# Mixer output stage: stores moved from SyncE to ScalarE and one product later, weight loads one tile sooner, inputs loaded and split in pieces, R times q in place

## The chip, the cores and the metric

The kernel runs on one core of a Trainium2 chip. The metric is the device time in microseconds of one execution of the program on that core. The core has TensorE (PE, with its weight loads shown apart as PEld), VectorE (DVE), ScalarE (ACT), GpSimd (POOL) and SyncE (SP). Each engine works through its own instructions in the order in which the built program holds them. SP here only issues DMA transfers, in one queue that is served in order.

## The reference

One layer with 128 context tokens and 2048 latent tokens, 2176 tokens in all, of 1024 channels in float32:

```
h = rmsnorm(x, norm1) * (1 + scale1) + shift1
z = h @ w_in
sc_b, sc_c, sc_x, q, k, v, o, g = jnp.split(z, idx, axis=-1)
y_sc = sc_b * conv3(sc_c * sc_x)                     # 512 channels
h_m, C, n, m = mlstm_bidir(q, k, v, g, C0, n0, m0)   # 4 heads of 128, chunks of 128 tokens
h_m = rmsnorm(h_m) * mh_norm * jax.nn.sigmoid(o)
x = x + gate1 * (jnp.concatenate([y_sc, h_m], axis=-1) @ w_out)
h2 = rmsnorm(x, norm2) * (1 + scale2) + shift2
a, gg = jnp.split(conv3(h2 @ w_up), 2, axis=-1)
x = x + gate2 * ((jax.nn.silu(gg) * a) @ w_down)
y = rmsnorm(x, final_norm)
```

(The reshapes, the context and latent calls and the per-head details are left out.) The change lies in the third to seventh of these lines.

## The kernel before

**Tiles and products.** Channels lie on the 128 partitions, tokens along the free dimension. Tokens are cut into six blocks `BL` of 384 (the last of 256). A float32 product is made of three matmuls: weights and inputs are split into a high part (`wh`, `hH`) and a low part (`wl`, `hL`), and `gemm` adds wh·hH, wh·hL and wl·hH for eight tiles of 128 channels. One such product (24 matmuls, called a product below) makes 128 output channels for one block. `load_w` brings one weight tile of 128x1024 from HBM (tile `wst`, two buffers), ACT makes `wh` from it (L110) and POOL makes `wl`.

**The stages.** After the norm and the first projections come the gate phase, `Sums` (backward states), then `Mix`, the output projection, and the FFN, which is the larger half of the time. In `Mix` there are 34 units, one for each of 17 chunks and two pairs of heads, with these stages:

- `load`: k, v, q and the backward state sb, by DMA (L724, L729, L793).
- `rows`: one row of 1024 numbers from HBM spread over all partitions into tile R (L799; four buffers). Half of R (index 0) is made into the weight matrix W, the other half (index 1) holds factors for q.
- `pre`: POOL adds a mask to W (L805), ACT takes the exponential (L809, four pieces).
- `first`: PE makes the scores in tile S, DVE multiplies the factors with q into a tile qs (L819) and the scores into W (L820, written as R).
- `second`: o2 is loaded; PE makes y from qs and the state, and from W and v (L831 and L833). DVE brings the forward state sf on (L837), takes the denominators den (L841 to L843), and with ACT makes hv (L848, L849), its sum of squares (L851, into hss) and its norm (L855).
- `third`: PE transposes hv into tile st (L861), DVE multiplies it into o2, shown as o (L863).
- `last`: o2 is stored to HBM as rows 4 to 7 of yD (L868).

`weave` sets the order in code. One step handles a stage each of several units, and then takes one product from `fill`: the q and o heads, the short convolution (which stores rows 0 to 3 of yD), and then the output projection:

```
for k, stage in ((-1, "second"), (0, "first"), (-3, "third"), (-4, "last"), (1, "pre"), (1, "load"), (2, "rows")):
```

**The output projection** (`out_proj`) takes the blocks in groups (0,1), (2,3), (4,5), and in each group eight output tiles m. For each m and block: a product into `acc`, then DVE adds gate1 times acc to a row tile that was loaded with x (L459, six buffers `row`), SP stores the row to xD (L461), ACT squares it (L466) and DVE adds the square to a sum (L467), from which `stats` makes the norm. The rows of the next tile are asked for one tile ahead (L436); the weights are asked for two tiles ahead, in `load_w`, which issues the DMA and the split together. The inputs of the product, `early[b]`, come from `load_y`: two DMAs of four rows each (tile `xt`, two buffers) and eight splits each on ACT and DVE. It is called for blocks 0 and 1 by the short convolution (its argument `then`), for block 2 at m = 4, for block 4 at m = 7, and for blocks 3 and 5 after a product of m = 7.

**What sets the order.** The code is written in an order, but the framework fixes each engine's order at build time with a scheduler of its own that may move instructions past each other. All DMAs are issued by SP, so a store that waits for its data holds back the loads behind it. When the stages of Mix are at their end, the last 16 products of the projection run on beside the first column sums of the FFN (`sums`, tile F, L255).

## Time and profile before

| what | us |
|---|---|
| median of 3 runs | 2561.06 |
| the runs' range | 2560.59 to 2562.93 |
| the profiled execution | 2561.92 |
| its span (first to last instruction) | 2560.1 |

Busy time of the engines by stretch of the profiled execution, with the mean granted clock of PE (1.00 is full speed) and the share of time in which the DMA engines were busy:

| us of the span | what runs | PE | DVE | ACT | POOL | clock | DMA |
|---|---|---|---|---|---|---|---|
| 0 to 220 | modulation, first norm | 199.72 | 165.74 | 75.02 | 79.50 | 0.97 | 0.77 |
| 220 to 640 | projections, gate phase | 409.77 | 132.72 | 119.55 | 102.70 | 0.99 | 0.50 |
| 640 to 720 | up to the first Mix units | 80.00 | 28.84 | 24.89 | 19.73 | 1.00 | 0.57 |
| 720 to 830 | Mix beside short convolution | 109.19 | 66.51 | 58.55 | 42.50 | 1.00 | 0.73 |
| 830 to 1150 | Mix beside output projection, then the projection's end | 286.90 | 217.72 | 165.40 | 118.89 | 0.96 | 0.79 |
| 1150 to 2090 | FFN up, convolution | 926.77 | 697.03 | 483.94 | 185.64 | 0.99 | 0.32 |
| 2090 to 2560 | FFN down, final norm | 457.19 | 337.79 | 185.48 | 13.69 | 0.98 | 0.66 |

In rows of the trace, `PE y L833 <- DVE R L820: 14.7, 8, 5.0` says that PE's instruction of line 833, which writes y, waited for DVE's of line 820, which wrote R: 14.7 us in all, 8 times, 5.0 at most. `acc<-hH,wh` names the output tile and the inputs. In a row of the timeline the first two numbers are start and duration in us, x2 stands for two like instructions shown as one, and `[1.54 <-DVE R L820]` is the idle time of the engine ahead of it and who ended it. SPq is SP's queue.

### The profile page before, as it was taken

The page shows a single profiled execution, that of the slowest core. Times are in us where ns is not written, and L with a number is a line of the kernel's source. Part 1 is how long each engine was busy: PE and PEld are TensorE (multiplying, and loading weights), DVE is VectorE, ACT ScalarE, POOL GpSimd, SP SyncE. Part 2 cuts the span into 40 slices and gives each one's busy share as a digit, 9 for nine tenths or more (in the row PEclk, how much of TensorE's full clock was granted, in tenths as well). Part 3 has the DMA queues.
Part 4 walks back from the last instruction along what each step waited for, and adds up shares of the span by engine and source line. Part 5 has one row for each costly group of instructions (what it writes and reads, how often), then busy time and mean ns, then how long its engine had stood idle before and what let it go on. Part 6 is the DMA issues. An engine that isn't in the chain of part 4 may idle for free.

```text
span 2560.1 us, 42529 instructions
## 1 busy us (share of the span) xinstructions
PE 2469.5 (96%) x16127; PEld 2364.6 (92%) x16127; DVE 1646.4 (64%) x2741; ACT 1112.8 (43%) x2035; POOL 562.6 (22%) x470
## 2 busy tenths in 40 slices
PE   8997999999999889899999999899999999999998
PEld 7997999999999889899999999788888889999998
DVE  3995432322356666778678666877777786787586
ACT  3521133322245555455455444555555554444342
POOL 2442223211233443322122111211221200000000
PEclk9999999999999999999999999999999999999999
DMA  7778623356567787775225222422222286767674
GB/s 281 240 268 292 232 83 119 100 170 176 182 190 244 250 266 228 250 257 173 83 79 174 74 83 83 146 100 84 91 99 83 87 260 207 248 204 224 187 218 134
DMA packets 281423, 444.60 MB, mean 174 GB/s; under 512 B 23282, under 2 KB 206722, under 8 KB 279554
## 3 DMA queue, kind: packets, MB, share of 16 engines
q1 hardware_dynamic: 281218, 441.88, 53.0%
q8 instruction: 127, 2.08, 0.3%
q14 instruction: 78, 0.64, 0.1%
HBM read 335.31 MB, written 106.48 MB: 173 GB/s over the span
## 4 chain that ended last, share of the span: by engine, by line
PE 74%; DVE 9%; DMA 8%; issue 3%; POOL 2%; ACT 2%; SPq 1%; DVEq 0%; POOLq 0%; ACTq 0%
PE pa L1004 7%; PE pa L1006 6%; PE pa L1005 6%; PE d L1163 6%; PE d L1164 6%; PE d L1162 6%; PE acc L204 5%; PE acc L206 5%; PE acc L205 5%; PE pb L1004 3%; PE pb L1006 3%; PE pb L1005 3%; DVE y L528 3%; PE pc L1004 2%; PE pc L1005 2%
## 5 line engine op out<-in xcount | busy, mean ns | idle before, releaser
L204 PE MATMUL acc<-hH,wh 128*128 128x384 f32 (+1 forms) x1536 | 515.1, 335 | 23.1 <-DVE cr L391 12.0
L205 PE MATMUL acc<-hL,wh 128*128 128x384 f32 (+1 forms) x1536 | 507.1, 330 | 0.0
L206 PE MATMUL acc<-hH,wl 128*128 128x384 f32 (+1 forms) x1536 | 507.0, 330 | 0.0
L1162 PE MATMUL d<-bh,wh 128*128 128x272 f32 x1232 | 357.9, 291 | 5.1 <-ACT bh L1091 5.1
L1163 PE MATMUL d<-bl,wh 128*128 128x272 f32 x1232 | 358.2, 291 | 0.9 <-DVE bl L1092 0.9
L1164 PE MATMUL d<-bh,wl 128*128 128x272 f32 x1232 | 358.4, 291 | 0.0
L1004 PE MATMUL pa<-tH,wh 128*128 128x288 f32 (+1 forms) x1056 | 348.5, 330 | 4.2 <-ACT c L1011 1.8
L1006 PE MATMUL pa<-tH,wl 128*128 128x288 f32 (+1 forms) x1056 | 346.8, 329 | 1.0 <-DVE wl L294 1.0
L1005 PE MATMUL pa<-tL,wh 128*128 128x288 f32 (+1 forms) x1056 | 347.3, 329 | 0.0
L294 POOL TENSOR_TENSOR wl<-st,wh 128x512 fp32r<-128x512 f32 x132 | 184.2, 1396 | 690.4 <-ACT wh L293 646.7
L113 POOL TENSOR_TENSOR wl<-wst,wh 128x512 fp32r<-128x512 f32 (+1 forms) x160 | 234.4, 1486 | 444.7 <-ACT wh L110 435.0
L204 PEld LDWEIGHTS acc<-hH,wh 128*128 128x128 f32 x1536 | 292.0, 190 | 25.8 <-DVE cr L391 13.3
L205 PEld LDWEIGHTS acc<-hL,wh 128*128 128x128 f32 x1536 | 292.5, 190 | 0.3 <-issue 0.2
L206 PEld LDWEIGHTS acc<-hH,wl 128*128 128x128 f32 x1536 | 291.9, 190 | 0.2 <-issue 0.2
L949 DVE SCALAR_TENSOR_TENSOR tt<-raw,fw,tt 128x127 f32<-128x127 f32 (+4 forms) x264 | 245.6, 951 | 4.2 <-ACT tt L955 3.1
L1162 PEld LDWEIGHTS d<-bh,wh 128*128 128x128 f32 x1232 | 233.8, 190 | 5.7 <-ACT bh L1091 5.6
L1163 PEld LDWEIGHTS d<-bl,wh 128*128 128x128 f32 x1232 | 234.1, 190 | 1.4 <-DVE bl L1092 1.2
L1164 PEld LDWEIGHTS d<-bh,wl 128*128 128x128 f32 x1232 | 233.9, 190 | 0.0
L1004 PEld LDWEIGHTS pa<-tH,wh 128*128 128x128 f32 x1056 | 198.5, 188 | 21.0 <-ACT c L1011 2.2
L1006 PEld LDWEIGHTS pa<-tH,wl 128*128 128x128 f32 x1056 | 199.3, 189 | 17.0 <-DVE wl L294 1.4
L1005 PEld LDWEIGHTS pa<-tL,wh 128*128 128x128 f32 x1056 | 198.8, 188 | 15.5
L293 ACT ACTIVATE wh<-s 128x512 fp32r<-128x512 f32 x176 | 110.8, 630 | 177.4 <-PE pc L1005 95.7
(235 smaller groups left out, 4842.5 us busy)
## 6 DMA issues: line engine op xcount, KB each, us to landing
st<-in_w_up SPq DMA_DIRECT2D x88, 512.0 KB, 4.5
us<-uD SPq DMA_DIRECT2D x48, 544.0 KB, 5.0
wst<-in_w_in SPq DMA_DIRECT2D x48, 512.0 KB, 4.1
uD<-tt SPq DMA_DIRECT2D x44, 544.0 KB, 2.7
R<-nD SPq DMA_DIRECT2D x34, 512.0 KB, 4.8
wm<-in_w_modr SPq DMA_DIRECT2D x32, 512.0 KB, 5.3
wst<-in_w_out SPq DMA_DIRECT2D x24, 512.0 KB, 4.3
st<-wsD SPq DMA_DIRECT2D x32, 384.0 KB, 3.3
```

The source lines that it names most:

```text
L113: G.tensor_sub(wl[:, a:a + n // 2], st[:, a:a + n // 2], wh[:, a:a + n // 2].bitcast(F32))
L204: PE.matmul(acc[:, :n], w_h, hH[:, k, :n], start=(k == 0), stop=False)
L205: PE.matmul(acc[:, :n], w_h, hL[:, k, :n], start=False, stop=False)
L206: PE.matmul(acc[:, :n], w_l, hH[:, k, :n], start=False, stop=(k == KT - 1))
L294: (G if on_pool else V).tensor_sub(wl, a, wh.bitcast(F32))
L949: V.scalar_tensor_tensor(o, i, w, o, op0=ALU.mult, op1=ALU.add)
L1004: PE.matmul(acc, wh[:, w], rh, start=(kk == 0 and i in (0, 1, 5)), stop=False, skip_group_check=True)
L1005: PE.matmul(acc, wh[:, w], rl, start=False, stop=False, skip_group_check=True)
L1006: PE.matmul(acc, wl[:, w], rh, start=False, stop=(kk == 3), skip_group_check=True)
L1162: PE.matmul(acc, wh[:, c], uh, start=(kk == 0), stop=False)
L1163: PE.matmul(acc, wh[:, c], ul, start=False, stop=False)
L1164: PE.matmul(acc, wl[:, c], uh, start=False, stop=(kk == KH - 1))
```

## The change

It has five parts.

- **Stores on ScalarE.** The 48 stores xD<-row and the 34 stores yD<-o are issued by ACT in place of SP, and pinned: `tc.keep_in_program_order` holds an instruction in the order of the code among the pinned ones of its engine. A row's store, its square and its sum (`close`) are written one product later than before.
- **Weights a tile sooner.** `load_w` is cut in two. `get_w` issues the DMA three tiles ahead; the split stays two tiles ahead and its ACT part is pinned.
- **Inputs in pieces.** `load_y` is cut into `get_y` (the DMAs) and `split_y` (half a block at a time). For blocks 2 to 5 the generator `next_y` issues them, one piece after each product from m = 2 on, as soon as the chunks are done. The second block of a group is split when the first block of the group before has had its last product. Blocks 0 and 1 still go through `load_y`.
- **In place.** R times q is written into R's second half in place of a tile qs.
- **Order of the stages.** `weave` writes the loads, the rows and a new stage `gate`, which loads o2, ahead of the others, and `second` still ahead of `first`.

```diff
--- before.py
+++ after.py
@@ -103,11 +103,21 @@
             if side and i % every == 0:
                 next(side, None)
 
-    def load_w(src, n=1024):
+    pin = tc.keep_in_program_order
+
+    def get_w(src, n=1024):
         st = wp.tile([P, WN], F32, name="wst", bufs=2)
         Q.dma_start(st[:, :n], src)
+        return st
+
+    def load_w(src, n=1024, st=None):
+        if st is None:
+            st = get_w(src, n)
+            keep = lambda ins: ins
+        else:
+            keep = pin
         wh = wp.tile([P, WN], F32R, name="wh")
-        S.activation(wh[:, :n], st[:, :n], AF.Copy)
+        keep(S.activation(wh[:, :n], st[:, :n], AF.Copy))
         wl = wp.tile([P, WN], F32R, name="wl")
         for a in (0, n // 2):
             G.tensor_sub(wl[:, a:a + n // 2], st[:, a:a + n // 2], wh[:, a:a + n // 2].bitcast(F32))
@@ -413,17 +423,44 @@
 
         done, early = set(), {}
 
-        def load_y(b):
+        def get_y(b):
 
             assert done >= set(chunks(b))
             t0, n = BL[b]
-            yH, yL = early[b] = h_pair()
+            yts = []
             for kh in range(2):
                 yt = xp.tile([P, 4, 384], F32, name="xt")
                 Q.dma_start(yt[:, :, :n], yD[4 * kh:4 * kh + 4, :, t0:t0 + n].rearrange("k p t -> p k t"))
-                for k in range(4):
-                    S.activation(yH[:, 4 * kh + k, :n], yt[:, k, :n], AF.Copy)
-                    V.tensor_sub(yL[:, 4 * kh + k, :n], yt[:, k, :n], yH[:, 4 * kh + k, :n].bitcast(F32))
+                yts.append(yt)
+            return yts
+
+        def split_y(b, yts, kh, keep=pin):
+
+            n = BL[b][1]
+            if kh == 0:
+                early[b] = h_pair()
+            yH, yL = early[b]
+            for k in range(4):
+                keep(S.activation(yH[:, 4 * kh + k, :n], yts[kh][:, k, :n], AF.Copy))
+                V.tensor_sub(yL[:, 4 * kh + k, :n], yts[kh][:, k, :n], yH[:, 4 * kh + k, :n].bitcast(F32))
+
+        def load_y(b):
+            yts = get_y(b)
+            for kh in range(2):
+                split_y(b, yts, kh, lambda ins: ins)
+
+        def next_y(grp, ready):
+
+            for b, may in zip(grp, ready):
+                while not done >= set(chunks(b)):
+                    yield
+                yts = get_y(b)
+                yield
+                for kh in range(2):
+                    while not may():
+                        yield
+                    split_y(b, yts, kh)
+                    yield
 
         def out_proj(grps, defer):
 
@@ -437,20 +474,35 @@
                     xs_.append(xr)
                 return xs_
 
+            def close(b, m, ss, xr):
+                t0, n = BL[b]
+                pin(S.dma_start(xD[m][:, t0:t0 + n], xr[:, :n]))
+                if m == 0:
+                    S.activation(ss[:, :n], xr[:, :n], AF.Square)
+                else:
+                    sq = sqp.tile([P, 384], F32, name="sq")
+                    S.activation(sq[:, :n], xr[:, :n], AF.Square)
+                    V.tensor_add(ss[:, :n], ss[:, :n], sq[:, :n])
+
             seq = [(g, m) for g in range(len(grps)) for m in range(KT)]
             ws = [load_w(I["w_out"][m]) for _, m in seq[:2]]
-            nx = load_r(grps[0], 0)
+            st = get_w(I["w_out"][seq[2][1]])
+            nx, behind = load_r(grps[0], 0), []
             for i, (g, m) in enumerate(seq):
-                grp = grps[g]
+                grp, final = grps[g], m == KT - 1
                 if m == 0:
                     sss = [ssp.tile([P, 384], F32, name="ss") for _ in grp]
+                    past = set()
+                    ny = iter(())
+                    if g + 1 < len(grps):
+                        ny = next_y(grps[g + 1], (lambda: True, lambda past=past, b=grp[0]: (b, KT - 1) in past))
                 w, xs_ = ws.pop(0), nx
                 if i + 1 < len(seq):
                     nx = load_r(grps[seq[i + 1][0]], seq[i + 1][1])
                 if i + 2 < len(seq):
-                    ws.append(load_w(I["w_out"][seq[i + 2][1]]))
-                if g + 1 < len(grps) and m == (4, 7)[min(g, 1)]:
-                    load_y(grps[g + 1][0])
+                    ws.append(load_w(None, st=st))
+                if i + 3 < len(seq):
+                    st = get_w(I["w_out"][seq[i + 3][1]])
                 for b, ss, xr in zip(grp, sss, xs_):
                     t0, n = BL[b]
                     acc = gemm(w, early[b], n)
@@ -458,21 +510,20 @@
                         a, e = a - t0, e - t0
                         V.scalar_tensor_tensor(xr[:, a:e], acc[:, a:e], modT[:, 16 + m, v:v + 1], xr[:, a:e],
                                                op0=ALU.mult, op1=ALU.add)
-                    Q.dma_start(xD[m][:, t0:t0 + n], xr[:, :n])
-                    if m == 0:
-                        S.activation(ss[:, :n], xr[:, :n], AF.Square)
-                    else:
-                        sq = sqp.tile([P, 384], F32, name="sq")
-                        S.activation(sq[:, :n], xr[:, :n], AF.Square)
-                        V.tensor_add(ss[:, :n], ss[:, :n], sq[:, :n])
-                    if m == KT - 1 and b == grp[1 - g] and g + 1 < len(grps):
-                        load_y(grps[g + 1][1])
+                    past.add((b, m))
+                    for x in behind:
+                        close(*x)
+                    behind = [(b, m, ss, xr)]
+                    if m >= 2:
+                        next(ny, None)
+                    if final and b == grp[-1]:
+                        run(ny)
+                        close(*behind.pop())
+                        if g == len(grps) - 1:
+                            defer.append(lambda: stats(grp, sss))
+                        else:
+                            stats(grp, sss)
                     yield
-                if m == KT - 1:
-                    if g == len(grps) - 1:
-                        defer.append(lambda: stats(grp, sss))
-                    else:
-                        stats(grp, sss)
 
 
         hs = {}
@@ -775,7 +826,7 @@
             def nothing(self):
                 pass
 
-            rows = pre = third = last = nothing
+            rows = pre = third = last = gate = nothing
 
         class Mix:
 
@@ -815,20 +866,18 @@
                 for h in range(2):
                     PE.matmul(psS[:, h * P:(h + 1) * P], self.k2[:, h], self.q2[:, h], start=True, stop=True)
                 if c >= 0:
-                    self.qs = mb.tile([P, 2, 2, P], F32, name="qs", bufs=2)
-                    V.tensor_tensor(self.qs, R[:, :, 1], bc(self.q2[:, :, None, :], [P, 2, 2, P]), op=ALU.mult)
+                    V.tensor_tensor(R[:, :, 1], R[:, :, 1], bc(self.q2[:, :, None, :], [P, 2, 2, P]), op=ALU.mult)
                 V.tensor_tensor(W, bc(psS[:, :256].rearrange("p (h t) -> p h t", h=2)[:, :, None, :],
                                       [P, 2, 2, P]), W, op=ALU.mult)
 
             def second(self):
                 c, hp, sf = self.c, self.hp, sfs[self.hp]
-                self.o2 = load2(mb, "o2", oD, c + 1, hp, 5)
                 y = pm.tile([P, 2, 512], F32, name="y", bufs=2)
                 for h in range(2):
                     for d in range(2):
                         o = y[:, h, d * 129:(d + 1) * 129]
                         if c >= 0:
-                            PE.matmul(o, self.qs[:, h, d], sf[:, h] if d == 0 else self.sb[:, h, 1],
+                            PE.matmul(o, self.R[:, h, 1, d], sf[:, h] if d == 0 else self.sb[:, h, 1],
                                       start=True, stop=False)
                         PE.matmul(o, self.R[:, h, 0, d], self.v2[:, h], start=c < 0, stop=True)
                 if 0 <= c < NL - 1:
@@ -863,9 +912,12 @@
                     V.scalar_tensor_tensor(o2[:, h], psT[:, h * P:(h + 1) * P], mhn[:, 2 * hp + h:2 * hp + h + 1], o2[:, h],
                                            op0=ALU.mult, op1=ALU.mult)
 
+            def gate(self):
+                self.o2 = load2(mb, "o2", oD, self.c + 1, self.hp, 5)
+
             def last(self):
                 hp, t0 = self.hp, (self.c + 1) * P
-                Q.dma_start(yD[4 + 2 * hp:6 + 2 * hp, :, t0:t0 + P].rearrange("h d t -> d h t"), self.o2)
+                pin(S.dma_start(yD[4 + 2 * hp:6 + 2 * hp, :, t0:t0 + P].rearrange("h d t -> d h t"), self.o2))
                 if hp:
                     done.add(self.c + 1)
 
@@ -873,7 +925,7 @@
 
             n = len(units)
             for i in range(-2, n + 4):
-                for k, stage in ((-1, "second"), (0, "first"), (-3, "third"), (-4, "last"), (1, "pre"), (1, "load"), (2, "rows")):
+                for k, stage in ((1, "load"), (2, "rows"), (-2, "gate"), (-1, "second"), (0, "first"), (-3, "third"), (-4, "last"), (1, "pre")):
                     if 0 <= i + k < n:
                         getattr(units[i + k], stage)()
                 if not -1 <= i < n + 3:
```

Line numbers move with it: the projection's row is L511 (was L459), its load L473, store L479, square L484, sum L485; in Mix, R's load is L850, the product R times q L869, W L870, the y store L920.

How the instructions stand is shown at three places. The first is VectorE around the W of one Mix unit beside the output projection. Rows name line, operation, output and inputs; L841, L842 and L890, L891 belong to the unit before it, and L459 or L511 are rows of the projection. Before:

```order
L459 SCALAR_TENSOR_TENSOR row<-acc,modT,row 128x384
L467 TENSOR_TENSOR ss<-ss,sq 128x384
L459 SCALAR_TENSOR_TENSOR row<-acc,modT,row 128x128
L459 SCALAR_TENSOR_TENSOR row<-acc,modT,row 128x256
L837 SCALAR_TENSOR_TENSOR sf_4979<-sf_4979,decB,sb 128x129 x2
L467 TENSOR_TENSOR ss<-ss,sq 128x384
L841 TENSOR_TENSOR den<-y,cols 128x4
L819 TENSOR_TENSOR qs<-R,q_9436 128x512
L842 SCALAR_TENSOR_TENSOR den<-y,den 128x4
L820 TENSOR_TENSOR R<-S,R 128x2x256
```

The same place on VectorE after the change:

```order
L511 SCALAR_TENSOR_TENSOR row<-acc,modT,row 128x384
L869 TENSOR_TENSOR R<-R,q_9448 128x2x256
L485 TENSOR_TENSOR ss<-ss,sq 128x384
L511 SCALAR_TENSOR_TENSOR row<-acc,modT,row 128x128
L511 SCALAR_TENSOR_TENSOR row<-acc,modT,row 128x256
L886 SCALAR_TENSOR_TENSOR sf_4979<-sf_4979,decB,sb 128x129 x2
L890 TENSOR_TENSOR den<-y,cols 128x4
L485 TENSOR_TENSOR ss<-ss,sq 128x384
L891 SCALAR_TENSOR_TENSOR den<-y,den 128x4
L870 TENSOR_TENSOR R<-S,R 128x2x256
```

The product with q moved six places up, ahead of the rows. The two sums of squares still stand ahead of W, but each now adds the square of an earlier product's row.

The second place is SyncE's queue, at the loads of the same unit. Before:

```order
L868 DMA yD<-o_8919 128x2x128
L724 DMA k_9432<-kD 128x2x128
L729 DMA v_9434<-vD 128x258
L724 DMA q_9436<-qD 128x2x128
L793 DMA sb<-sD 128x516
L724 DMA o_9472<-oD 128x2x128
L461 DMA xD<-row 128x384
L799 DMA R<-nD 128x1024
L724 DMA k_9519<-kD 128x2x128
L729 DMA v_9521<-vD 128x258
L868 DMA yD<-o_9070 128x2x128
```

After the change:

```order
L850 DMA R<-nD 128x1024
L473 DMA row<-in_x 128x384
L775 DMA k_9358<-kD 128x2x128
L780 DMA v_9360<-vD 128x258
L775 DMA q_9362<-qD 128x2x128
L844 DMA sb<-sD 128x516
L775 DMA o_9368<-oD 128x2x128
L850 DMA R<-nD 128x1024
L775 DMA k_9444<-kD 128x2x128
L780 DMA v_9446<-vD 128x258
L775 DMA q_9448<-qD 128x2x128
```

No store is left between the loads; a row load (L473) stays among them.

The third place is ScalarE in the same step (R with cols is the exponential, wh the weight split, hv with hss the norm of h). Before:

```order
L809 ACTIVATE R<-R,cols 128x128 x2
L855 ACTIVATE hv<-hv,hss 128x128 x2
L809 ACTIVATE R<-R,cols 128x128
L466 ACTIVATE sq<-row 128x384
L809 ACTIVATE R<-R,cols 128x128
L110 ACTIVATE wh<-wst 128x1024
L466 ACTIVATE sq<-row 128x384
L848 ACTIVATE hv<-y,den 128x128
```

After the change:

```order
L904 ACTIVATE hv<-hv,hss 128x128 x2
L920 DMA yD<-o_9048 128x2x128
L479 DMA xD<-row 128x384
L484 ACTIVATE sq<-row 128x384
L860 ACTIVATE R<-R,cols 128x128 x3
L120 ACTIVATE wh<-wst 128x1024
L479 DMA xD<-row 128x384
L484 ACTIVATE sq<-row 128x384
L897 ACTIVATE hv<-y,den 128x128
```

Two stores of rows and one of o stand among ACT's work of this step.

## The prediction

> **What bounds the kernel now.** I read the page first, then the waits of the matrix engine in the part that the change touches, then one wait back to its cause on the other engines.
>
> ```profile
> span 2560.1 us, 42529 instructions
> PE 2469.5 (96%) x16127; PEld 2364.6 (92%) x16127; DVE 1646.4 (64%) x2741; ACT 1112.8 (43%) x2035; POOL 562.6 (22%) x470
> ```
>
> PE is busy 2469.5 of 2560.1 us, so the whole kernel can give back at most the 90.6 us in which PE stands still, and whatever it loses to a lower clock. The change adds and removes no matmul. It touches Mix and the output projection (about 720 to 1150 us), so the next view is who PE waits for between 800 and 1150 us (engine, line, what it waited for; total us, times, longest):
>
> ```profile
> PE y L833 <- DVE R L820: 14.7, 8, 5.0
> PE acc L204 <- DVE row L459: 5.9, 2, 5.0
> PE st L127 <- DVE o L863: 2.9, 1, 2.9
> PE st L127 <- DVE rc L130: 2.9, 1, 2.9
> PE acc L204 <- DVE cr L391: 1.8, 2, 1.5
> PE st L127 <- DVE ss L467: 1.4, 1, 1.4
> PE st L861 <- DVE o L863: 1.4, 1, 1.4
> ```
>
> These sum to 31.0 us, and every one is a wait for DVE. The largest is the weight matrix W of a Mix unit (L820, written into tile R), which the second matmul of that unit (L833) needs. The timeline of PE shows where four of these gaps lie (start, length, instruction, idle time before it and who ended it):
>
> ```profile
> 837.22 0.49 PE L833 MATMUL y<-v,R 128*128 128x129 f32 x2 [1.54 <-DVE R L820]
> 856.64 0.80 PE L833 MATMUL y<-v,R 128*128 128x129 f32 x2 [4.98 <-DVE R L820]
> 904.02 0.79 PE L833 MATMUL y<-v,R 128*128 128x129 f32 x2 [2.49 <-DVE R L820]
> 932.27 0.49 PE L833 MATMUL y<-v,R 128*128 128x129 f32 x2 [2.23 <-DVE R L820]
> ```
>
> DVE is not full there. I follow the last gap back on DVE:
>
> ```profile
> 926.02 0.56 DVE L467 TENSOR_TENSOR ss<-ss,sq 128x384 f32<-128x384 f32 x1 [3.56 <-ACT sq L466]
> 926.49 0.74 DVE L459 SCALAR_TENSOR_TENSOR row<-acc,modT,row 128x128 f32<-128x128 f32 x2
> 927.14 0.61 DVE L837 SCALAR_TENSOR_TENSOR sf<-sf,decB,sb 128x129 f32<-128x129 f32 x2
> 928.53 1.34 DVE L467 TENSOR_TENSOR ss<-ss,sq 128x384 f32<-128x384 f32 x1 [0.78 <-ACT sq L466]
> 929.80 0.15 DVE L841 TENSOR_TENSOR den<-y,cols 128x4 f32<-128x4 f32 x1
> 929.87 1.67 DVE L819 TENSOR_TENSOR qs<-R,q 128x512 f32<-128x512 f32 x1
> 931.47 0.15 DVE L842 SCALAR_TENSOR_TENSOR den<-y,den 128x4 f32<-128x4 f32 x1
> 931.54 0.68 DVE L820 TENSOR_TENSOR R<-S,R 128x512 f32<-128x512 f32 x1
> ```
>
> W at 931.54 stands behind two sums of squares (L467), which nobody needs yet and which idled DVE for 3.56 and 0.78 us, and behind a product for the next unit (qs, 1.67 us). Without those 6.01 us W would have been far ahead of PE, which needed it only 2.23 us sooner. The sums wait for squares on ACT, so I look there:
>
> ```profile
> 923.92 0.69 ACT L809 ACTIVATE R<-R,cols 128x128 f32<-128x128 f32 x2 [2.26 <-POOL R L805]
> 925.48 0.51 ACT L466 ACTIVATE sq<-row 128x384 f32<-128x384 f32 x1
> 927.03 1.06 ACT L110 ACTIVATE wh<-wst 128x1024 fp32r<-128x1024 f32 x1 [0.75 <-DMA wst<-in_w_out]
> 928.00 0.51 ACT L466 ACTIVATE sq<-row 128x384 f32<-128x384 f32 x1
> ```
>
> ACT had the squares in its queue behind an exponential, which waited 2.26 us for a mask sum on POOL, and behind a weight split, which waited 0.75 us for a DMA. Both hang on loads, and the loads stand in one queue (SP) behind stores. Over the whole stretch from 830 to 1030 us (the first row is DVE's waits, the second POOL's) and for SP's own waits from 800 to 1130 us:
>
> ```profile
> DVE ss L467 <- ACT sq L466: 30.4, 21, 3.6
> POOL R L805 <- DMA R<-nD: 20.7, 8, 6.5
> SPq L436 <- DMA xD<-row: 32.5, 15, 4.7
> SPq L868 <- DVE hv L849: 27.4, 11, 4.1
> SPq L461 <- DVE row L459: 18.1, 11, 3.6
> SPq L868 <- DVE o L863: 17.8, 7, 7.0
> ```
>
> So the loop is: a store (L461, L868) stops SP until DVE is done, loads of R and weights go late, POOL and then ACT wait, the squares go late, DVE waits for them, W goes late, PE waits.
>
> **The change part by part.** PE's order stays, but for a few rows at its end, so every microsecond must come out of the waits above.
>
> *Stores on ScalarE.* 48 xD and 34 yD stores leave SP, and the 27.4 + 18.1 + 17.8 = 63.3 us that SP stood in front of them go with them. On ACT each xD store and its square come one product later than the row they need, and each yD store a step after its o. The trace has no DMA issued by ACT. Nearest is SP's issue of the same store (ns min/median/max):
>
> ```profile
> L461 SPq DMA_DIRECT2D xD<-row x48: 319/363/1576, 845.0 to 1119.1; - x48
> 830.00:1030.00 200.00, 179.36 (x1138) 176.44 (x1139) 128.13 (x336) 104.21 (x305) 82.63 (x71) 0.97 0.78 247
> ```
>
> 82 issues by 0.363 us are 29.8 us more on ACT, with bounds of 82 by 0.319 = 26.2 and 82 by 1.576 = 129 us. Its cover is ACT's idle time: in the second row (window, then busy us of PE, PEld, DVE, ACT and POOL, granted clock, DMA share, GB/s) ACT is busy 104.21 of 200 us. I take the median and price it at nothing on the path. If half of the 29.8 us had no cover it would cost 15 us, and that is a rival below.
>
> *Squares one product later.* The 30.4 us that DVE idles ahead of L467 should mostly go, because ACT gets a whole matrix product to make the square. One sum still stands ahead of W in DVE's new order, but it no longer reads a row just made.
>
> *R times q held in place, a step's place earlier.* The 32 products stay the same size. The nearest rows are the qs row above (1.67 us, stretched) and W's 0.68 us, which writes the same strided shape, so the product itself costs neither more nor less. Its place ahead of W is what counts: in most steps it moves ahead of the sf updates or the row, into time in which DVE waits anyhow.
>
> *Loads first in a step, o loaded in a stage of its own, weights a tile sooner.* The count of loads is unchanged. They only move ahead, past the stores. What may still stop SP is the row load, which waits for an older xD store to land: 32.5 us in 15 waits. That store is now issued later, so I expect this wait to stay about as it is.
>
> *Inputs in pieces, pinned.* The 48 splits on ACT and 48 on DVE (eight of each for each of six blocks) stay the same work. For blocks 2 to 5 they are spread over two places, each after its load has been asked for an earlier product. Blocks 0 and 1 are still loaded from the short convolution as before.
>
> **The sum.** Of the 14.7 us for W, the gap of 1.54 us at 837 lies in the short convolution and stays. At 856 the split inputs came late (the load had to wait for a store by the short convolution), and I leave 1 us of the 4.98. The other 12.2 us go. Of the two waits for o (2.9 + 1.4) I take 3.0, since o stands behind the same sums. Of the statistics' wait for ss (1.4) I take 1.0. The two waits for rows (5.9 us), rc's 2.9 us and cr's 1.8 us are not touched: at 1086 the row stood behind a block of F sums that fills DVE:
>
> ```profile
> 1085.38 0.45 DVE L255 TENSOR_TENSOR F<-F 128x288 f32<-128x288 f32 x1
> 1085.75 1.00 DVE L459 SCALAR_TENSOR_TENSOR row<-acc,modT,row 128x384 f32<-128x384 f32 x2
> 1086.41 0.69 PE L204 MATMUL acc<-hH,wh 128*128 128x384 f32 x1 [4.95 <-DVE row L459]
> ```
>
> The gaps also cost clock. Same columns as in the window row above, 0.83 being the granted clock:
>
> ```profile
> 850.00:860.00 10.00, 5.02 (x28) 4.83 (x27) 8.41 (x20) 6.77 (x22) 7.04 (x6) 0.83 0.78 250
> 900.00:910.00 10.00, 7.51 (x42) 7.32 (x41) 7.18 (x17) 5.09 (x16) 4.49 (x5) 0.83 0.89 284
> 950.00:960.00 10.00, 9.91 (x59) 9.41 (x60) 7.75 (x21) 5.91 (x19) 4.76 (x4) 0.83 0.90 271
> ```
>
> PE's busy time in them by the 0.17 that is missing: (5.02 + 7.51 + 9.91) x 0.17 = 3.8 us, or 5.1 us if the whole windows count. I take 3.0, for a little of it stays. The sum is 12.2 + 3.0 + 1.0 + 3.0 = 19.2 us. The profiled execution took 2561.92 us (span 2560.1 plus 1.8 around it), 0.86 above the median of 2561.06 us. So 2542.7 for that execution, and **2541.9** against the median.
>
> The windows with 0.83 follow gaps of 4.98 and 2.49 us, and the third one follows 2.87 us (the wait for o). [...]
>
> **Rivals.** *All of it goes.* If DVE is freed so far that the 31.0 us and the whole 5.1 us of clock go, the time is 2561 - 36 = 2525 us. For it: all waits are for DVE, and DVE has 36% idle time in the window row. Against it: rc, cr and the F block do not hang on the moved work.
>
> *The DMA engines take over.* They are busy 0.78 of the time in the stretch and 0.89 and 0.90 in two of the windows above. A stage that runs a tenth faster asks the same bytes in less time. If R and the weights then land just as late, only the part that the squares and qs gave (about a third of 19.2 us) is left: 2555 us. For it: R already kept POOL waiting 20.7 us. Against it: SP stood still in front of stores while those loads were due. [...]
>
> *ScalarE becomes the late engine (slower).* The stores and splits are pinned, so ACT cannot pass them. If they reach the head of ACT's queue before DVE has made their row or o, or if the issue time falls between den and hv, then everything behind waits: exponentials for W, squares, hv, weight splits. Price: the 29.8 us of issue lie on the path and the 19.2 us are still gained: 2561 + 29.8 - 19.2 = 2572 us. It decides from the point where a store's wait plus its issue exceeds ACT's idle share, about 0.48 of a step.
>
> *The scheduler's order gives nothing*: the squares wait as long, one product later, and the time stays at 2561.
>
> **How the numbers follow.** Forecast (2534 to 2550) 50%, all of it 19%, DMA 16%, nothing gained 6%, ScalarE late 9%. The range leaves out half of the slow case and the best part of the fast one: 2521 to 2563 us. About 0.2% (5.1 us) is what a measurement of this kernel can tell from no change, so faster means under 2555.9: the first two and just over half of the DMA case, 78%. Within 0.2%: the rest of that case and the idle one, 13%. Slower: 9%.
>
> **What would show it.** Right: PE's wait for W under 4 us in total, DVE's wait for squares under 10 us, SP with no wait for hv, o or row, no granted clock of 0.83 between 860 and 1010 us, and the 4.95 us gap at the F block still there. Wrong: ACT waiting in front of its stores, DVE waiting in the early R-times-q product for a load, R still late on POOL, or PE waiting for split inputs at a group's first product.

## The result and the profile after

The changed kernel takes 2589.59 us (median of 4 runs, 2584.3 to 2590.88) against 2561.96 us before in the same runs. The ratio is 1.0104, with a 95% interval of 1.0088 to 1.0120: slower by about 1%, where 2541.9 us had been forecast. The profiled execution is the fastest of the four, 2584.3 us.

The page's first two lines after the change (span; busy time of each engine):

```profile
span 2582.5 us, 42533 instructions
PE 2476.9 (96%) x16127; PEld 2372.0 (92%) x16127; DVE 1647.8 (64%) x2741; ACT 1113.7 (43%) x2035; POOL 564.9 (22%) x470
```

Of the 22.4 us that the span grew, 7.4 are PE's busy time for the same 16127 matmuls, beside a mean granted clock of 0.981 against 0.987 before, and 15.0 are idle time. To see where, I take three marks in both traces: the first scores of Mix (705.5 us before, 706.2 after), the last row of the projection (L459, now L511), and the end. From the first mark to the second it is 413.1 us before and 439.8 after, and all else is within 6 us. This stretch is called **the stage** below, and its length in each profile is worked out in the same way.

Who PE waits for from 800 to 1150 us, after the change (engine, line, what it waited for; total us, times, longest):

```profile
PE y L882 <- DVE R L870: 14.8, 6, 6.2
PE acc L214 <- DVE row L511: 9.3, 3, 7.4
PE acc L214 <- ACT hH L444: 6.0, 1, 6.0
PE st L137 <- DVE ss L485: 5.7, 2, 2.8
PE acc L214 <- ACT wh L120: 5.3, 2, 5.0
```

The wait for W stands where it stood (14.7 us before), in fewer and longer pieces. New ones have come beside it: ScalarE's splits, for inputs (6.0) and weights (5.0 at one place). (The prediction's list left out 2.2 us of waits for ScalarE, before the change, in the rows `PE pc L1004 <- ACT tH L278: 1.5`, `PE st L235 <- ACT rb L237: 0.4` and `PE pa L1004 <- ACT tH L278: 0.3`; not every wait was for VectorE.) The same views as in the prediction for the engines behind them, VectorE, GpSimd and ScalarE from 830 to 1030 us and SyncE from 800 to 1130 us:

```profile
DVE R L869 <- DMA q<-qD: 24.8, 9, 4.6
DVE ss L485 <- ACT sq L484: 18.8, 15, 2.5
...
POOL R L856 <- DMA R<-nD: 59.6, 14, 7.7
...
ACT R L860 <- POOL R L856: 34.8, 17, 5.0
...
SPq L473 <- DMA xD<-row: 55.5, 20, 8.3
...
SPq L775 <- DMA yD<-o: 20.8, 5, 7.0
SPq L844 <- DVE sf L886: 20.5, 6, 6.8
SPq L110 <- POOL wl L123: 20.4, 10, 3.4
```

SyncE's waits in front of stores are gone, as they must be. In their place it waits in front of loads: row loads for a row store to land (32.5 us before), loads of o, sb and weights for a tile that is still in use. VectorE's wait for squares fell from 30.4 to 18.8 us, but a new one of 24.8 us stands ahead of R times q. GpSimd's wait for R nearly tripled (20.7 before), and ScalarE's wait for the mask sum doubled (17.3 before).

The largest gap for W shows how they hang together. These are rows of the timelines of SyncE, VectorE, ScalarE and PE, in this order, with start, length and the idle time ahead:

```profile
915.33 0.38 SPq L850 DMA_DIRECT2D R<-nD  x1
924.13 0.33 SPq L473 DMA_DIRECT2D row<-in_x  x1
...
935.00 0.70 DVE L869 TENSOR_TENSOR R<-R,q 128x512 f32<-128x512 f32 x1 [3.80 <-DMA q<-qD]
937.80 0.56 DVE L485 TENSOR_TENSOR ss<-ss,sq 128x384 f32<-128x384 f32 x1 [2.11 <-ACT sq L484]
...
941.35 0.67 DVE L870 TENSOR_TENSOR R<-S,R 128x512 f32<-128x512 f32 x1
...
935.18 0.41 ACT L860 ACTIVATE R<-R,cols 128x128 f32<-128x128 f32 x1 [4.78 <-POOL R L856]
...
942.08 0.80 PE L882 MATMUL y<-v,R 128*128 128x129 f32 x2 [6.17 <-DVE R L870]
```

SyncE issues nothing for 8.8 us in front of a row load. Then q and R for a later unit are late, VectorE stands at the product R times q, ScalarE at the exponential, and the squares, W and PE come after both. This looked like the whole story, and most of the experiments were made to test it. It does not explain the loss, as the last two experiments show.

The gaps go with lost clock as before the change (window, busy us of PE, PEld, DVE, ACT and POOL, granted clock, DMA share, GB/s):

```profile
830.00:1030.00 200.00, 172.79 (x1071) 169.54 (x1070) 120.53 (x316) 100.04 (x296) 76.54 (x67) 0.93 0.75 238
850.00:860.00 10.00, 7.18 (x37) 6.87 (x38) 4.81 (x14) 4.54 (x15) 2.06 (x2) 0.66 1.02 352
940.00:950.00 10.00, 7.92 (x42) 7.93 (x43) 5.04 (x13) 1.84 (x8) 4.37 (x4) 0.71 0.71 227
```

### The profile page after: what moved, and what is told of

It reads as the page before. It is cut to its first block, busy times and chain, and to the rows that moved or that the text cites. A ratio compares the mean times of both kernels' runs of the same rounds, so it can differ in the third digit from the quotient of the medians.

```text
span 2582.5 us, 42533 instructions
## 1 busy us (share of the span) xinstructions
PE 2476.9 (96%) x16127; PEld 2372.0 (92%) x16127; DVE 1647.8 (64%) x2741; ACT 1113.7 (43%) x2035; POOL 564.9 (22%) x470
## 4 chain that ended last, share of the span: by engine, by line
PE 69%; DMA 9%; DVE 6%; ACT 2%; issue 2%; POOL 2%; SPq 1%; ACTq 0%; DVEq 0%; POOLq 0%
PE pa L1056 7%; PE pa L1058 7%; PE pa L1057 7%; PE acc L214 5%; PE acc L215 5%; PE acc L216 5%; PE d L1215 5%; PE d L1216 5%; PE d L1214 5%; PE pb L1056 3%; PE pb L1058 3%; PE pb L1057 3%; DMA R<-nD 2%; PE pc L1056 2%; PE pc L1057 2%
## 5 line engine op out<-in xcount | busy, mean ns | idle before, releaser
L214 PE MATMUL acc<-hH,wh 128*128 128x384 f32 (+1 forms) x1536 | 518.5, 338 | 36.8 <-DVE cr L401 10.1
L214 PEld LDWEIGHTS acc<-hH,wh 128*128 128x128 f32 x1536 | 294.7, 192 | 40.1 <-DVE cr L401 11.0
```

Source lines behind the costliest of these rows:

```text
L214: PE.matmul(acc[:, :n], w_h, hH[:, k, :n], start=(k == 0), stop=False)
```

## The experiments

The medians, the interval of the ratio to before, and the length of the stage in one profile (413.1 us before). Each group of runs had its own runs of before, whose medians lie between 2559.8 and 2562.0 us, so runs of different groups are best compared by their ratios:

| run | what differs | us | 95% interval of the ratio | stage |
|---|---|---|---|---|
| after | | 2589.6 | 1.0088 to 1.0120 | 439.8 |
| e1 | after, qs tile | 2588.2 | 1.0081 to 1.0114 | 440.3 |
| e2 | after, row closed at once | 2577.9 | 1.0041 to 1.0095 | 431.8 |
| e3 | after, old order of stages | 2596.9 | 1.0111 to 1.0160 | 456.0 |
| e4 | after, all stores on SyncE | 2565.7 | 1.0008 to 1.0030 | 415.5 |
| e5 | after, row stores on SyncE | 2578.7 | 1.0043 to 1.0089 | 433.2 |
| e6 | after, o stores on SyncE | 2579.3 | 1.0042 to 1.0086 | 435.8 |
| e7 | after, seven o tiles | 2585.0 | 1.0059 to 1.0105 | 438.2 |
| e8 | after, stores not pinned | 2583.5 | 1.0054 to 1.0114 | 439.3 |
| e9 | after, seven row tiles | 2590.0 | 1.0086 to 1.0122 | 434.0 |
| e10 | after, stores on GpSimd | 2594.9 | 1.0113 to 1.0145 | 447.0 |
| e11 | e8, loads in code order | 2574.9 | 1.0031 to 1.0067 | 430.0 |
| e12 | e4, loads in code order | 2569.8 | 1.0015 to 1.0044 | 427.9 |
| f1 | after, five R tiles | 2582.6 | 1.0073 to 1.0108 | 439.4 |
| f2 | e4, five R tiles | 2576.3 | 1.0052 to 1.0082 | 429.6 |
| f3 | before, stores on ScalarE | 2589.6 | 1.0102 to 1.0132 | 440.4 |
| f4 | e4, row closed at once | 2569.2 | 1.0019 to 1.0048 | 422.9 |
| g1 | e8, every order as in e4 | 2567.5 | 1.0023 to 1.0054 | 425.1 |
| g2 | e8, SyncE's order as in e4 | 2578.0 | 1.0057 to 1.0096 | 433.7 |

### One part undone at a time

**e1.** The product goes into a tile of its own again.

```diff
-V.tensor_tensor(R[:, :, 1], R[:, :, 1], bc(self.q2...
+self.qs = mb.tile([P, 2, 2, P], F32, name="qs", bufs=2)
+V.tensor_tensor(self.qs, R[:, :, 1], bc(self.q2...
```

> After with one part undone: the product R times q goes into its own tile qs again, which puts it back directly ahead of W on VectorE. Theory A (early product: in place, the product stands at the head of VectorE before its q has landed, 33 us of waits for the q and o loads from 800 to 1180 us, and W and the rows behind it are late): the waits of the product for a load go under 5 us, PE's wait for W falls from 14.8 to under 8 us, and the time falls from about 2589 to about 2572 us or lower. Theory B (row buffers: the stores one product later keep the six row tiles, SyncE stands 57 us in front of row loads, and everything after it is late): unchanged, 2585 to 2592, since q and R land as late as before.

Two waits after the change, from 720 to 1150 us, that the runs below are held against:

```profile
ACT R L860 <- POOL R L856: 60.4, 30, 5.0
...
POOL R L856 <- DMA R<-nD: 109.0, 24, 9.3
```

2588.2 us, no gain. VectorE waits for no q any more, and PE's wait for W in the stretch from 720 to 1150 us falls from 17.6 to 9.8 us. But ScalarE's wait for the mask grows from 60.4 to 69.2 us, and PE's wait for the statistics rises to 10.1. Theory A falls.

**e2.** `close` runs in the product's own step.

```diff
-for x in behind: close(*x)
-behind = [(b, m, ss, xr)]
+close(b, m, ss, xr)
```

> After with one part undone: store, square and sum of a row follow in the same product again (stores still on ScalarE). Theory B (row buffers): SyncE's wait of row loads for row stores falls from 57 to about 32 us as before the change, POOL's wait for R from 73 to under 40, and the time to about 2572 us or lower. Theory A (early product): SyncE's row waits may fall, but VectorE still waits over 20 us for q ahead of the product, and the time stays above 2580. Theory C (ScalarE is late: 40 us of waits for rows at its head): worse than after, above 2592, since the stores meet their rows sooner.

2577.9 us. SyncE's wait of row loads falls to 31.3 us as theory B says, with less than the gain it asked for, and GpSimd's wait for R stays at 106.4 us (109.0 after the change). Theory C's sign is wrong.

**e3.** The old order of the stages.

```diff
-((1, "load"), (2, "rows"), (-2, "gate"), (-1, "second"), ... (1, "pre"))
+((-1, "gate"), (-1, "second"), ... (1, "pre"), (1, "load"), (2, "rows"))
```

> After with one part undone: the stages of a step in the old order (second, first, third, last, pre, load, rows), o2 loaded right ahead of second. Theory D (loads written first meet buffers that are not free yet: SyncE stands 35.6 us for sb and 33 us for o and q loads from 720 to 1150 us): these waits fall to the 8 and 22 us of before, and the time to about 2572 or lower. Theories A and B: the time stays above 2582.

2596.9 us, slower still, with intervals that overlap: if the new order of stages does anything with the stores away from SyncE, it helps. The o loads now wait 91.8 us for o stores. Theory D falls.

**e4.** Both stores back on SyncE; all else as after.

```diff
-pin(S.dma_start(xD...))   and   pin(S.dma_start(yD...))
+Q.dma_start(xD...)        and   Q.dma_start(yD...)
```

> After with one part undone: both stores are issued by SyncE again, still one product later for rows. Theory C (ScalarE is late because pinned stores wait at its head): ScalarE's waits for rows fall from 40 to under 15 us and the time to about 2565 or lower. Theory B (row buffers): SyncE now stands in front of stores and of row loads, and the time stays at 2585 or goes higher, up to 2600.

2565.7 us: nearly all of the loss is gone, as theory C says, but not by its reason. ScalarE's waits for rows in the stretch from 720 to 1150 us, 31.0 and 9.4 us after the change, are 32.0 and 7.1 us here. What fell is its wait for the mask:

```profile
ACT R L860 <- POOL R L856: 44.1, 24, 6.8
ACT hv L897 <- DVE den L892: 37.7, 25, 3.6
ACT sq L484 <- DVE row L511: 32.0, 17, 3.9
```

SyncE stops in this run too, in front of the stores and of the row loads:

```profile
SPq L920 <- DVE hv L898: 38.6, 17, 4.1
SPq L473 <- DMA xD<-row: 34.8, 17, 4.2
SPq L479 <- DVE row L511: 23.7, 14, 3.5
...
SPq L920 <- DVE o L912: 22.1, 10, 4.9
```

### Which store, and is it the store's lateness?

In the traces I paired each store with what it stores. After the change an o store is issued a median 14.5 us after its o is made, since the pin holds it in its place a step later; on SyncE (before, e4) it was 0.03 us. A late store keeps its tile (from 720 to 1150 us after the change, row loads wait 57.0 us for row stores and o loads 33.3 us for o stores), so e5 to e9 test tiles and lateness.

**e5, e6.** One of the two stores on SyncE, the other on ScalarE (the diff of e4, halved).

> After, but the 48 row stores are issued by SyncE again; the 34 o stores stay on ScalarE, pinned. The runs so far: moving both back gives 2565.7 against 2589.6, and on ScalarE an o store is issued a median 14.5 us after its o is made (0.03 on SyncE), a row store 0.97 us after its row, at most 14.7 (0.15 and 6.2 on SyncE). Theory E (rows: late row stores keep the row tiles, SyncE waits 57 us in front of row loads): these waits fall to about 35 us and the time to 2570 or lower. Theory F (o: late o stores keep o's five tiles and the inputs of the next blocks): the time stays above 2582, with the o loads' wait of 33 us and the inputs' wait of 15.5 us.

> After, but the 34 o stores are issued by SyncE again; the 48 row stores stay on ScalarE, pinned. Theory F (o): the o loads' wait falls from 33 us to under 10, the gap of 6 us for the inputs at 853 us goes, and the time falls to 2570 or lower. Theory E (rows): the time stays above 2582 and SyncE's wait of row loads for row stores above 50 us. If each half gives about half, both this and the run with rows on SyncE come out near 2577.

2578.7 and 2579.3: each gives about half. Neither store is the cause alone.

**e7.** More tiles for o.

```diff
-load2(mb, "o2", oD, self.c + 1, self.hp, 5)
+load2(mb, "o2", oD, self.c + 1, self.hp, 7)
```

> After, with seven o tiles in place of five; both stores stay on ScalarE. Theory F in its form that the late o store keeps a tile which an o load then waits for: SyncE's wait of o loads for o stores falls from 33 us to under 8 and the time to about 2575. In its other form (only the inputs of the next blocks are late), and by theory E: above 2584.

2585.0, where theory F in the form that blames the tile asked for about 2575. But the o loads still wait 22.7 us (33.3 after the change, under 8 expected): the run takes away a third of the wait only, so it speaks against this form and does not rule it out.

**e8.** Both stores on ScalarE, without the pin.

> After, with both stores on ScalarE but not pinned, so that the scheduler may put them sooner. Theory G (the pin holds the stores at a place that is too late): o stores are issued less than 6 us after their o, and the time falls to 2575 or lower. Otherwise (ScalarE's work ahead of a store delays it wherever it stands, or its place doesn't matter): 2585 to 2592.

2583.5. The stores are now issued a median 0.03 us after their row or o, at most 4.9, and the time falls by 6 us, with intervals that overlap. So lateness is a small part at most, and theory G falls. (The pin sets an instruction behind the one written just ahead of it on its engine, pinned or not, which is more than the section on the change says.) SyncE waits in front of the loads longer than after the change (57.0 and 33.3 us in this stretch), and ScalarE's wait for the mask is no shorter:

```profile
SPq L473 <- DMA xD<-row: 65.9, 27, 5.4
SPq L775 <- DMA yD<-o: 65.9, 22, 5.8
...
ACT R L860 <- POOL R L856: 67.4, 25, 5.0
```

**e9.** One more row tile; room for it is made by one buffer less at the kernel's start.

```diff
-tc.tile_pool(name="rp", bufs=6)   ... name="wm", bufs=5
+tc.tile_pool(name="rp", bufs=7)   ... name="wm", bufs=4
```

> After, with seven row tiles in place of six (and four in place of five buffers for the modulation weights at the kernel's start, which makes the room; what that costs lies in the first 220 us and is read there). Theory H (a row load meets a row tile whose store has not landed, and stops SyncE's whole queue): a tile more gives a product's time (about 8 us) more, so SyncE's wait of row loads for row stores falls from 57 to under 15 us, POOL's wait for R from 109 to under 70, and the time to 2578 or lower. If the row loads only stand where something else would stop SyncE next: the wait goes and the time stays at 2584 to 2592.

2590.0. The first scores of Mix start at 715.4 us, so 9.2 us of it are the start's. The stage is 5.8 us shorter than after, in one profile each. The wait of row loads went as expected, and others took its place (57.0, 33.3 and 35.0 us after the change for these; the last is for the weights' two rows):

```profile
SPq L775 <- DMA yD<-o: 48.8, 14, 5.5
...
SPq L110 <- POOL wl L123: 34.3, 17, 3.1
...
SPq L110 <- ACT wh L120: 15.6, 7, 5.9
SPq L473 <- DMA xD<-row: 15.0, 11, 3.8
```

GpSimd's wait for R is 93.4 us, where theory H asked for under 70, and the time did not fall. Theory H falls: a tile does little for a queue that stops at the next one.

### ScalarE, or any other queue?

**e10.** Both stores on GpSimd, not pinned.

```diff
+G.dma_start(xD...)   and   G.dma_start(yD...)
```

> After, with both stores on GpSimd, not pinned (its DMA queue is a third one). Theory I (what costs is ScalarE's own time and place: issue time and waits in its queue): ScalarE is rid of the stores as when SyncE has them, and the time is 2570 or lower. Theory J (what costs is that the stores leave SyncE's queue, whichever engine takes them: loads are then ordered ahead and meet tiles that are not free): the time stays at 2578 or higher, with SyncE's waits for row and o stores above 80 us in all.

2594.9: ScalarE is rid of the stores, and the kernel is slower still. GpSimd now waits in front of stores itself, and an issue takes it 0.562 us (rows) or 0.731 us (o) at the median, so this run is not a clean one:

```profile
POOL yD L920 <- DVE o L912: 56.5, 20, 6.0
...
POOL xD L479 <- DVE row L511: 34.1, 16, 6.4
```

It gives theory I no support. SyncE waits 155.6 us in front of row and o loads (73.0 and 82.6), as theory J asks, which points to what the stores leave, not to where they go.

**e11, e12.** The loads of k, v, q, sb, o, R and of the rows are pinned in the order of the code, once with the stores on ScalarE and once on SyncE.

> After, with the loads of Mix and of the rows held in the order of the code on SyncE, stores on ScalarE, not pinned. To be compared with the next run, which has the same order of loads and its stores on SyncE. Theory J (order of the loads): the two are within 6 us of each other. Theory K (a second queue's transfers lengthen the loads: q landed in 4.6 us with the stores on ScalarE, 3.4 with them on SyncE): this one is slower than the next by over 12 us.

> As the run before, with the stores on SyncE, not pinned. Theory J: within 6 us of the run before. Theory K: over 12 us faster than it, near 2565.

2574.9 and 2569.8: 5 us apart and the intervals overlap, where e8 and e4 are 18 apart. With nearly one order of these loads (6 of the 318 in the traces, all rows, stand elsewhere), the queue of the stores matters little. That speaks for theory J, in an order that is not the best one. The rest of SyncE's queue and the other engines were not held, so it is a hint and no proof.

### The ring of R tiles

**f1, f2.** R of a unit can be loaded only when the unit four before has read its tile. A fifth tile loosens that (the room is that of qs).

```diff
-name="R", bufs=4
+name="R", bufs=5
```

> After, with five R tiles in place of four (the room is that of the qs tile, which the change gave up). Theory L (the ring: R of unit u is loaded only after y of unit u-4, so whatever stops SyncE just then delays the load, the mask, the exponential, and all that stands behind the exponential on ScalarE): POOL's wait for R falls from 109 to under 40 us, ScalarE's wait for the mask from 60 to under 25, and the time to 2570 or lower. Theory M (the other stops count: rows, o, weights, and R only happens to be late with them): R's waits fall, and the time stays above 2580.

> After with both stores on SyncE and five R tiles. Theory L: as with four tiles the ring is the tightest place left, so the time falls below the 2565.7 of four tiles, to 2550 to 2560. Theory M: 2562 to 2570, as with four.

2582.6 and 2576.3. In f1 both waits fall, though not as far as theory L asks, GpSimd's from 109.0 us and ScalarE's from 60.4. But ScalarE's wait for GpSimd's part of the norm (hss) rises, from 23.6 us:

```profile
POOL R L856 <- DMA R<-nD: 46.7, 17, 5.7
...
ACT hv L904 <- POOL hss L902: 50.4, 33, 4.9
ACT R L860 <- POOL R L856: 37.3, 21, 4.5
```

The time falls by 7 us only, with intervals that overlap, and in f2 it rises by 11 against e4. Theory L falls: in f2 the order is another one again, with the exponentials further ahead, and ScalarE waits 64.0 us for the mask.

### The move alone, and the order alone

**f3.** Before, with the engine of both stores changed and nothing else.

> Before, with nothing changed but that ScalarE issues both stores, pinned where the code has them. If the move of the stores alone makes the loss: 2580 or higher, with SyncE stopped in front of row and o loads and ScalarE's wait for the mask above 50 us. If it does so only together with the rest of the change (loads first, in place, weights sooner): 2568 or lower.

2589.6: the whole loss, with the order that the scheduler makes for this code. ScalarE's wait for the mask is 74.4 us (40.1 before, in this stretch).

**f4.** e4 with the row closed at once.

> After with both stores on SyncE and each row's store, square and sum in its own product again; what is left of the change is the weights a tile sooner, the inputs in pieces, R times q in place and the order of the stages. If the squares one product later are worth their part of the prediction (VectorE's wait for squares 26 against 33 us): slower than the 2565.7 of the run with the delay, 2568 or higher. If not: 2558 to 2566, VectorE's wait for squares as before.

2569.2 against 2565.7, intervals overlapping. The squares' delay is worth 3.5 us at the most likely, not shown to be more than nothing. VectorE's wait for squares is 24.6 us with it undone and 26.5 with it.

**g1, g2.** The code of e4 and of e8 differs in the engine of 82 stores, but the scheduler then places other instructions differently too. Beside the stores, at least 55 on SyncE, 62 on ScalarE, 90 on VectorE and 12 on GpSimd have to be moved to turn one built order into the other; counted by place, as in the expectation of g2, it is more. g1 takes the code of e8 and holds every other instruction of these four engines, in Mix and the projection, in e4's order; only the 82 stores differ (and a few of PE's instructions: 18 of its 16127 matmuls in the traces). The traces of e4 and g1 show the same order on these four engines, row by row. g2 holds SyncE's alone.

```diff
+ORDERS = {"SP": (...), "Activation": (...), "DVE": (...), "Pool": (...)}   # g2: "SP" only
+def fix_order(tc):
+    at = {i.name: i for i in tc.nc.cur_bb.bb.instructions}
+    for order in ORDERS.values():
+        for a, b in zip(order, order[1:]):
+            tc.add_manual_dep(at[f"I-{b}"], f"I-{a}", info, reason="order")
```

> After with both stores on ScalarE, not pinned, and every other instruction of the four engines held in the order that the scheduler gave to the run with both stores on SyncE (2565.7 us). Theory J (the loss is the order that the scheduler makes once the stores have left SyncE's queue: with the queue free in its reckoning, loads and what uses them are put ahead of their time): about 2565, not above 2570. Theory K (the loss is on the chip: stores that go beside the loads from a second queue, and loads that no store holds back any more): 2578 or higher, with POOL's wait for R near 100 us. In between: both.

> After with both stores on ScalarE, not pinned, and only SyncE's loads held in the order of the run with stores on SyncE; ScalarE, VectorE and GpSimd as the scheduler puts them (112, 179 and 19 instructions stand elsewhere than in that run). Theory N (the loads' order makes the loss: row, weight and o loads ahead of R, k, v and q): at most 2572. Theory O (the order of the work makes it: masks, exponentials and products with q put ahead of their data): 2578 or higher.

g1: **2567.5 us**, with the stores on ScalarE. g2: 2578.0. Theory J holds for most of the loss, and theory N holds at most in part. From e8 to g1 PE's waits from 720 to 1150 us fall from 45.0 to 38.2 us, and no more than 4.2 of this is the wait for W (20.6 to 16.4): rows give 6.3 (8.4 to 2.1) and ss 4.1 (5.5 to 1.4), while new small ones come. PE's busy time for the same matmuls falls by 5.6 us (2477.3 to 2471.7). What makes g1 worth a look are its waits from 720 to 1150 us, SyncE's and then ScalarE's and GpSimd's:

```profile
SPq L473 <- DMA xD<-row: 73.9, 19, 7.0
SPq L775 <- DMA yD<-o: 43.3, 11, 7.1
...
ACT R L860 <- POOL R L856: 47.4, 24, 6.0
...
POOL R L856 <- DMA R<-nD: 72.0, 18, 9.4
```

SyncE stands in front of row and o loads for 117 us, longer than after the change (90) and not much less than in e8 (132), and yet the kernel is 22 us faster than the one and 16 us faster than the other. The length of SyncE's stops does not set the time. Nor did the stores take the stops with them: in e4, with the same order, it is 84 us in front of stores and 35 us in front of row loads, 119 us in all. ScalarE's wait for the mask is back near e4's 44.1.

Theory K is not quite ruled out. Transfers land later in g1 than in e4 (medians from issue to landing, 720 to 1150 us): q after 4.5 us against 3.4, o stores after 5.0 against 2.8. The medians are 1.8 us apart, the ratios 1.0039 and 1.0019, which is 5 us, with intervals that overlap; in one profile each the stage is 9.6 us longer. What the move costs by itself is thus open between nothing and some 10 us, and it is no gain.

## Why the prediction was wrong

**The step that failed** is the first sentence of its second part: "PE's order stays, but for a few rows at its end, so every microsecond must come out of the waits above." PE's order did stay. The orders of the other four engines did not, and the prediction priced that at nothing. The scheduler orders by its own reckoning of when things are ready. When the stores leave SyncE's queue it orders anew, and some two hundred instructions stand elsewhere (e8 against e4), on engines that the change does not name. The chain of runs sizes it: with e4's order, the move of the stores costs 1.8 us (2567.5 against 2565.7) or 5 by the ratios, with intervals that overlap; with the scheduler's own order and no pin it costs 17.8 or 17 (e8). So 11 to 16 us are order. SyncE's order gives 2 to 5.5 of them (e8 to g2, intervals overlapping) and that of ScalarE, VectorE and GpSimd about 10 (g2 to g1, intervals apart). The pin gives the 5 to 6 us from e8 to the change, with intervals that overlap. The last 4 to 5 us, e4 against before, are what the other parts cost together.

This is the loss. That the forecast gain of 19.2 us stayed out as well is the second half of the same sentence: "the waits above" did not go with the stores. The term at fault is the 63.3 us of SyncE, which the prediction took to vanish; with one order held they came back in front of the loads (e4 119 us, g1 117 us).

**Which rows of the order** was not tried one by one. One count looked like an answer: how far ahead of its own unit's norm (L904) a unit's first exponential stands on ScalarE. Counted in units over the last 20, with ScalarE's wait for the mask from 720 to 1150 us:

| run | exponential ahead by | wait for the mask, us | median us |
|---|---|---|---|
| e4 | 3.65 | 44.1 | 2565.7 |
| g1 | 3.65 | 47.4 | 2567.5 |
| after | 3.80 | 60.4 | 2589.6 |
| e8 | 3.85 | 67.4 | 2583.5 |
| g2 | 3.95 | 61.3 | 2578.0 |
| f3 | 4.00 | 74.4 | 2589.6 |
| before | 3.70 | 40.1 | 2562.0 |
| e2 | 3.70 | 50.2 | 2577.9 |
| e3 | 3.65 | 69.4 | 2596.9 |
| f1 | 4.00 | 37.3 | 2582.6 |
| f2 | 3.95 | 64.0 | 2576.3 |

In the first six rows the count parts the two fast runs from the four slow ones, though it does not rank the four. The last five rows break it: e3 has the count of e4 and is the slowest run of all, and f1 has the shortest wait in the table and is still at 2582.6. That an exponential which stands earlier than its R can land holds up what is behind it on ScalarE (squares, hv, splits) is seen at the gap at 942 us, where ScalarE stood 4.78 us ahead of the exponential. That this makes the loss is argued, and not shown; which rows of the order cost the 11 to 16 us stays open.

Point by point:

- **Stores leave SyncE, 63.3 us of its waits go.** They went, and others came in front of the loads. As a gain the move is worth nothing: g1 has no wait in front of a store on SyncE and is no faster than e4. The loop that the prediction drew, from a stopped SyncE to a waiting PE, did not open by moving the stores; whether a SyncE that never stops would gain anything, no run shows. SyncE runs ahead of need by much: before the change the R of the unit whose W ran at 931.54 us was asked for at 902.60, 29 us earlier.
- **The row load's wait "to stay about as it is".** 32.5 became 55.5 us. It is the wait that moved, from in front of the store to in front of the load that needs it. With most of it gone the time was the same (e9, where others took its place).
- **82 issues at 0.363 us, hidden.** Right. They took 0.327 us (rows) and 0.377 us (o) at the median, and g1, which has all of them on ScalarE, is 1.8 us from e4, which has none (5 by the ratios, intervals overlapping).
- **Squares a product later.** VectorE's wait fell from 30.4 to 18.8 us, not below 10. Its worth was at most a few us (f4), and with the stores on ScalarE the delay cost 11.7 (e2), with intervals that overlap.
- **R times q in place.** Priced at nothing because it moves "into time in which DVE waits anyhow". It became a wait of its own (24.8 us), and taking it away gave nothing (e1).
- **W: 12.2 of 14.7 us go.** None went. **Clock: 3.0 us back.** Lost instead: 0.97 to 0.93 from 830 to 1030 us.
- **The 4.95 us at the F block stay.** The same place now has one of 7.4 us: the row's add at 1122.03 stands behind 2.54 us of F work and more. Of the prediction's four signs of being wrong, three came: VectorE waits for a load at R times q (24.8 us), R is late on GpSimd (59.6 us), and PE waits 6.0 us for split inputs at the first product of block 1.
- **Rivals.** ScalarE as the late engine had the right sign, but its price was 29.8 us of issue time, and g1 rules that out; of its other road, stores that wait at the head of ScalarE's queue, e4 shows no trace (ScalarE's waits for rows are 31.0 us with the stores and 32.0 without). The DMA rival had loads as late as before for want of bandwidth, at 2555 us; the mean DMA share from 830 to 1030 us is 0.75 after and 0.78 before, which gives it no support. With the order held, g1 against e4, the move alone shows no gain, but 1.8 us more.

No version here beats before. e4 is the nearest, and its interval lies above 1.

## What to carry to other kernels

Where a scheduler fixes the order at build time, moving instructions to another engine is two changes: the move, and a new order everywhere. Hold the order and make the move alone before believing a mechanism; here that one run showed what ten runs on tiles, pins and queues could not. A long wait on a queue that runs well ahead need not be a cost either: here, taking it away let the queue reach its next wait sooner (in e9, row loads waited 15.0 us in place of 57.0, and o loads 48.8 in place of 33.3). And hold a count that seems to explain the time against every run, not only those that suggested it.

## What the runs showed of the hardware

A store issued by ScalarE takes its queue about as long as on SyncE: 0.327 us for a row and 0.377 for o after the change, 0.363 and 0.371 on SyncE before it (medians). On GpSimd they take 0.562 and 0.731 us (e10). The rows for the two stores after the change (ns min/median/max, first and last start):

```profile
L479 ACTq DMA_DIRECT2D xD<-row x48: 326/327/748, 845.7 to 1146.6; - x48
L920 ACTq DMA_DIRECT2D yD<-o x34: 366/377/430, 748.9 to 1044.0; - x34
```

The granted clock was 0.66 in the 10 us window with PE's gap of 6.01 us, and 0.71 in the window with the gap of 6.17 us. It was 0.66 also from 960 to 970 us, beside a gap of 2.83 us, and before the change from 1050 to 1060 us, beside one of 2.85 us, while the three gaps of 4.98, 2.49 and 2.87 us in the prediction stood beside 0.83. So the length of the gap does not tell the clock by itself here. The 7.4 us of extra busy time for the same matmuls is a third of the loss in the span.
